# A fixed order for all engines in the heads part of a hybrid block, with the recurrence's growth on VectorE

## The chip, the cores and the metric

One core of one Trainium2 chip runs the kernel. The metric is device microseconds of one execution; three runs of the kernel before gave 1198.59, 1198.85 and 1199.2 us (median 1198.85). Engines are named as in the profile: PE is TensorE's matmul, PEld its weight load, DVE is VectorE, ACT ScalarE, POOL GpSimd, SP SyncE (it issues the weight DMAs).

## The reference, cut to what matters

A block of 512 tokens (with 16 meta tokens: 528) and 1024 channels: half a SwiGLU FFN, a mixer, another half FFN, all in float32. The mixer is the part that is changed.

```python
u = rms_norm(h, mix_norm)
z = u @ w_in                 # 42 blocks of 128 columns
y_a = hgrn2_bidir(...)       # 4 heads: gated linear recurrence, both directions
y_b = axial_gqa(...)         # 8 query heads, 2 key heads, rotary positions, softmax over 528 keys
mixed = sigmoid(zgate_a) * (y_a @ w_up_a) + sigmoid(zgate_b) * (y_b @ w_up_b)
h = h + mixed @ w_out
```

## The kernel before, in words

Activations lie with channels in partitions and tokens in the free dimension. Every float32 product by a weight is made of three matmuls in a reduced format: `Weights.parted` splits a block of weights into a rounded part `whi` (ACT, L84) and the rest `wlo` (DVE, L85), the activations are split the same way into `xh`, `xl`, and `group` (L197) sums hi*hi, hi*lo and lo*hi over eight slices in a PSUM bank. Such matmuls are called weight matmuls here.

The mixer with heads has five strands:

- The main strand: `zcols` computes 128 columns of `z` after another (24 weight matmuls of 512 tokens, or 48 of half the width for 528 tokens) and evicts them on DVE.
- The queries (`queries_rest`): a reciprocal root by Newton steps on DVE, the rotation, a split into `qst`.
- The attention, 32 times (4 pairs of heads, 2 heads each, 4 blocks of 128 queries). `score`: four matmuls fill the one tile `S` (two PSUM banks, a single buffer); DVE takes the maximum (`nm`, L699), ACT scales it (`nr`, L701) and takes the exponentials with their sum (`pr`, L704), DVE inverts the sum (`sm`, L706), ACT scales (`pr`, L707). `turned`: five transposes into `at` and `am`, `ph` on ACT (L722), `pl` on DVE (L723). After four of them `product` multiplies by the values (L734, L735).
- The recurrence of a head (`gla_head`): seven levels m = 1, 2, ... 64. In a level ACT copies `ks` (L884), PE multiplies (L888, tile `gs`, one bank), and `grow` updates: POOL multiplies the query half of Z (L875), DVE the key half (L877), POOL the factors `tot` (L879); DVE writes the level into `A` (L892).
- Its end (`gla_out`): transposes of Z (L916, L921), two sums of states (L926, L928), the output (L942), four squares on ACT (L946), a Newton root on DVE (L561 to L563), four scalings on ACT (L949), a transpose (L953).

Who is next: PE's order is fixed while the program is made. `Interleave` holds a clock that grows by given costs per eight, or 24, weight matmuls, and a strand's step is put into PE's order when its own time (a constant such as LAT_S0 = 3.2 after the last step, LAT_G = 3.5 for a level, LAT_N = 7.0 for the root) has come. `need` runs strands until a condition holds, without main work between: before the queries of head pair hd the scores of hd - 2 must be out, before the recurrence's inputs of hd its head hd - 2 must be done (two buffers of Z). ACT, DVE and POOL are not in this order: a list scheduler with priorities orders them. All engines run their own queues in order, each instruction waiting for its semaphores.

Of the kernel before, what the change touches and what calls it, by code (L numbers as in the profile page):

```python
# [30 lines left out]
OFFSET = 300  # L31
# [20 lines left out]
class Weights:  # L52


    def __init__(self, nc, pool, ahead):
        self.nc, self.pool, self.ahead = nc, pool, ahead
        self.todo, self.ready = [], []
        self.plain = self.into = self.extra = None

# [3 lines left out]
    def emit(self, halves=False):  # L63
# [12 lines left out]
        self.parted(self.pool, [(c, raw[:, c]) for c in cuts])  # L76

# [47 lines left out]
    def fill(self):  # L125
        while self.todo and len(self.ready) <= self.ahead:
            self.emit()
# [6 lines left out]
class Interleave:  # L134
# [3 lines left out]
    def __init__(self, tc, offset):  # L138
        self.tc, self.offset = tc, offset
        self.t, self.chains, self.events, self.done = 0.0, [], {}, set()  # L140

    def add(self, gen):
        self.chains.append([gen, 0.0, None])

    def signal(self, name, latency):
        self.events[name] = self.t + latency

    def ready(self, ch):
        if ch[2] is not None:
            return max(ch[1], self.events.get(ch[2], float("inf")))  # L150
        return ch[1]

    def step(self, ch):
        ch[2] = None
        with self.tc.high_priority(self.offset):
            got = next(ch[0], None)
        if got is None:
            self.chains.remove(ch)
        elif isinstance(got, str):
            ch[2] = got  # L160
        else:
            cost, latency = got
            self.t += cost
            ch[1] = self.t + latency

    def pump(self):
        while True:
            ch = min(self.chains, key=self.ready, default=None)
            if ch is None or self.ready(ch) > self.t:
                return  # L170
            self.step(ch)

    def main(self, cost):
        self.t += cost
        self.pump()

    def need(self, name):
        while name not in self.done:
            ch = min(self.chains, key=self.ready)
            self.t = max(self.t, self.ready(ch))  # L180
            self.step(ch)


def block_kernel(tc, xT, wg1, wu1, wd1, w_in, wup, wout, wg2, wu2, wd2, params,
                 cosT, sinT, masks, ident_in, out):
    nc = tc.nc
    act, dve, pe, pool = nc.scalar, nc.vector, nc.tensor, nc.gpsimd
# [14 lines left out]
    with (tc.tile_pool(name="persist", bufs=1) as sp, tc.tile_pool(name="wts", bufs=1) as wp,  # L202
# [271 lines left out]
        with tc.tile_pool(name="f1", bufs=1) as ft:  # L474
# [45 lines left out]
            plan += tiles[:EARLY] + tiles[KT:KT + 1] + tiles[EARLY:KT] + tiles[KT + 1:]  # L520
# [7 lines left out]
        with tc.tile_pool(name="mix", bufs=1) as mp, tc.manual_schedule(engines={pe.engine}):  # L528
            il = Interleave(tc, OFFSET)

            def zcols(n):

                if n == T:
                    outs = [(bank("mm")[:, :c.stop - c.start], c) for c in FULL]
                else:
                    outs = [(bank("mm"), slice(0, SEQ))]
                group(outs, W.next(), um, il.main)
                return outs

            def scaled(dst, outs, sign=None):  # L540
                for o, cols in outs:
                    if sign is None:
                        dve.tensor_tensor(dst[:, cols], o, R[:, cols], ALU.mult)
                    else:
                        dve.scalar_tensor_tensor(dst[:, cols], o, sign, R[:, cols], ALU.mult, ALU.mult)

            def tmp():
                return mp.tile([P, TP], F32, name="tm", tag="tm", bufs=3)[:, :T]

            def rsqrt(x, scale, eps, shape, tag):  # L550


                x0 = x
                x, y, a = (mn.tile(shape, F32, name=n, tag=n, bufs=b)
                           for n, b in ((f"x{tag}", 1), (f"y{tag}", 2), (f"a{tag}", 1)))
                dve.tensor_scalar(x, x0, scale, eps, ALU.mult, ALU.add)
                yi = y.bitcast(I32)
                dve.tensor_scalar(yi, x.bitcast(I32), 1, None, ALU.logical_shift_right)
                dve.tensor_scalar(yi, yi, -1, 0x5F3759DF, ALU.mult, ALU.add)
                for _ in range(3):  # L560
                    dve.tensor_tensor(a, y, y, ALU.mult)  # L561
                    dve.scalar_tensor_tensor(a, a, -0.5, x, ALU.mult, ALU.mult)
                    dve.scalar_tensor_tensor(y, a, 1.5, y, ALU.add, ALU.mult)  # L563
                return y
# [21 lines left out]
            with tc.tile_pool(name="heads", bufs=1) as hp, tc.tile_pool(name="small", bufs=1) as mn:  # L586
# [6 lines left out]

                def qtmp():
                    return hp.tile([P, TP], F32, name="tq", tag="tq", bufs=1)[:, :T]

                def rope(z, n, cn, cs):

                    zs = qtmp()
                    dve.stream_shuffle(zs[:, :n], z[:, :n], swap)  # L600
                    dve.scalar_tensor_tensor(z[:, :n], z[:, :n], par[:, cn:cn + 1], cosS[:, :n], ALU.mult, ALU.mult)
                    dve.scalar_tensor_tensor(zs[:, :n], zs[:, :n], par[:, cs:cs + 1], sinS[:, :n], ALU.mult, ALU.mult)
                    dve.tensor_tensor(z[:, :n], z[:, :n], zs[:, :n], ALU.add)

# [3 lines left out]
                def keys():  # L608
                    kz = tmp()
                    scaled(kz, zcols(T))  # L610
                    ksq = tmp()
                    act.activation(ksq, kz, AF.Square)
                    il.signal("keys", LAT_SQ)
                    inputs["keys"] = kz, ksq

                def keys_rest():
                    kz, ksq = inputs["keys"]
                    krs = tmp()
                    for cols in FULL:
                        o = bank("mm")  # L620
                        n = cols.stop - cols.start
                        pe.matmul(o[:, :n], kones, ksq[:, cols], start=True, stop=True)
                        act.activation(krs[:, cols], o[:, :n], AF.Sqrt, bias=eps, scale=1.0 / 64)  # L623
                    for cols in FULL:
                        dve.reciprocal(krs[:, cols], krs[:, cols])
                    rope(kz, T, C_KN, C_KNS)
                    dve.tensor_tensor(kz, kz, krs, ALU.mult)
                    for kv in range(2):
                        s, d = slice(kv * 64, kv * 64 + 64), slice(64 - kv * 64, 128 - kv * 64)
                        kh = hp.tile([P, TP], F32R, name=f"kh{kv}")[:, :T]  # L630
                        kl = hp.tile([P, TP], F32R, name=f"kl{kv}")[:, :T]
                        act.copy(kh[s], kz[s])
                        act.copy(kh[d], kz[s])
                        dve.tensor_tensor(kl[s], kz[s], kh[s].bitcast(F32), ALU.subtract)
# [4 lines left out]
                def values():  # L639
                    vz = tmp()  # L640
                    scaled(vz, zcols(T))
                    inputs["values"] = vz
                    il.signal("values", LAT_V)

                def values_rest():
                    vz = inputs["values"]
# [3 lines left out]
                    for cs in (slice(0, 4), slice(4, 5)):  # L650
                        ov = bank("mm").rearrange("p (c v) -> p c v", c=4)
                        w, n = (4, P) if cs.start == 0 else (1, META)
                        for c in range(w):
                            c0 = (cs.start + c) * P
                            pe.transpose(ov[:n, c, :], vz[:, c0:c0 + n], ident)
                        for kv in range(2):
# [451 lines left out]
```

## Time and profile before

| | |
|---|---|
| median of 3 runs | 1198.85 us |
| the profiled execution | 1199.99 us, span 1198.1 us |
| PE busy | 1169.3 us (98% of the span) |
| DVE, ACT, POOL busy | 853.7, 581.4, 186.1 us |
| chain that ended last, by engine | PE 86%, DVE 8%, ACT 2%, issue 2% |

The busy shares say that PE sets the pace; what can be won or lost by an order are the times in which PE waits, and the time in which its clock is granted at the lower of its two levels. The part with heads lies at 381 to 706 us of the span: `rstd` before it ends at 381 us, the transpose L953 of the last head at about 706 us. A busy matmul is modelled at its end, so a short wait can hide in it.

### The profile page before, as it was taken

Reading aid. Unit: us, or ns where it says so; the run is one execution under the profiler, and the core shown is the slowest. Engines: PE = TensorE matmul, PEld = TensorE weight load, DVE = VectorE, ACT = ScalarE, POOL = GpSimd, SP = SyncE. Lnnn points to the kernel's source line nnn. Section 1 sums busy time; section 2 is a strip of 40 time slices with the busy share of each in tenths; the row PEclk is TensorE's granted clock in tenths of the full one; section 3 lists DMA queues with packets and bytes.
Section 4 is the critical chain, followed back from the end, with each engine's and each line's share of the span. In section 5 each row is a group of like instructions: output and inputs, shape, how many; then the busy total and the mean of one; then the engine's idle time right before and its main releaser. Section 6 shows DMA issues by size and latency. Waiting matters only on the chain.

```text
span 1198.1 us, 19412 instructions
## 1 busy us (share of the span) xinstructions
PE 1169.3 (98%) x7765; PEld 1070.7 (89%) x7765; DVE 853.7 (71%) x1349; ACT 581.4 (49%) x982; POOL 186.1 (16%) x153
## 2 busy tenths in 40 slices
PE   8999999999999999899999999999999999999998
PEld 8999999999999788878888788888878998998997
DVE  7988848847956769687677835454788956866863
ACT  5545525524645476656547533334444633543541
POOL 1001001001102023233232410122001101101100
PEclk9999999999999999999999999999999999999999
DMA  6133322323223221111111113232413232333213
GB/s 233 63 95 128 102 89 89 114 80 106 71 67 119 81 71 36 53 37 53 36 54 36 62 45 114 85 117 90 156 53 128 97 102 97 109 98 110 89 54 123
DMA packets 34235, 106.22 MB, mean 89 GB/s; under 512 B 3937, under 2 KB 4321, under 8 KB 34145
## 3 DMA queue, kind: packets, MB, share of 16 engines
q1 hardware_dynamic: 33984, 104.44, 26.0%
q8 instruction: 61, 1.00, 0.3%
q0 software_dynamic: 160, 0.54, 0.1%
q14 instruction: 30, 0.24, 0.1%
HBM read 102.87 MB, written 2.10 MB: 88 GB/s over the span
## 4 chain that ended last, share of the span: by engine, by line
PE 86%; DVE 8%; ACT 2%; issue 2%; DMA 1%; SPq 0%; POOL 0%; ACTq 0%; DVEq 0%
PE mm L197 34%; PE mm L374 14%; PE at L374 9%; PE at L197 5%; PE am L197 5%; PE gs L374 4%; PE S L197 4%; PE am L374 2%; DVE wlo L85 2%; PE gs L888 2%; PE S L695 1%; PE mm L734 1%; PE mm L942 1%; PE at L719 1%; ACT whi L84 1%
## 5 line engine op out<-in xcount | busy, mean ns | idle before, releaser
L84 ACT CAST whi<-raw 128x1024 fp32r<-128x1024 f32 (+2 forms) x220 | 189.4, 862 | 290.5 <-PE mm L197 125.8
L85 DVE TENSOR_TENSOR wlo<-raw,whi 128x1024 fp32r<-128x1024 f32 (+2 forms) x220 | 223.5, 1018 | 28.8 <-ACT whi L84 23.1
L197 PE MATMUL mm<-xh,whi 128*128 128x512 f32 (+1 forms) x504 | 166.3, 363 | 4.7 <-ACT xh L278 1.4
L197 PE MATMUL mm<-xl,whi 128*128 128x512 f32 (+1 forms) x504 | 160.3, 352 | 1.3 <-DVE xl L279 1.3
L197 PE MATMUL mm<-xh,wlo 128*128 128x512 f32 (+1 forms) x504 | 159.4, 350 | 0.0
L116 POOL TENSOR_TENSOR sums<-raw 128x512 f32<-128x512 f32 x36 | 57.9, 1609 | 494.8 <-DVE wlo L85 494.8
L84 ACT CAST whi<-sums 128x1024 fp32r<-128x1024 f32 x72 | 75.4, 1050 | 62.4 <-DVE sums L111 21.2
L85 DVE TENSOR_TENSOR wlo<-sums,whi 128x1024 fp32r<-128x1024 f32 x72 | 87.5, 1217 | 25.2 <-ACT whi L84 25.1
L197 PEld LDWEIGHTS mm<-xh,whi 128*128 128x128 f32 x504 | 89.6, 191 | 17.5 <-ACT tm L623 1.8
L197 PEld LDWEIGHTS mm<-xh,wlo 128*128 128x128 f32 x504 | 89.3, 190 | 12.7 <-issue 0.2
L197 PEld LDWEIGHTS mm<-xl,whi 128*128 128x128 f32 x504 | 89.3, 190 | 11.8 <-DVE xl L279 2.2
L875 POOL TENSOR_TENSOR Z<-Z,tot 128x512 f32<-128x512 f32 x32 | 47.3, 1477 | 157.8 <-PE gs L888 125.1
L197 PE MATMUL mm<-hh,wlo 128*128 128x256 f32 (+1 forms) x218 | 63.0, 334 | 0.0
L197 PE MATMUL mm<-hh,whi 128*128 128x256 f32 (+1 forms) x218 | 62.9, 333 | 0.1
L197 PE MATMUL mm<-hl,whi 128*128 128x256 f32 (+1 forms) x218 | 62.9, 332 | 0.0
L374 PE MATMUL mm<-xl,whi 128*128 128x264 f32 (+1 forms) x216 | 61.3, 284 | 0.0
L374 PE MATMUL mm<-xh,whi 128*128 128x264 f32 (+1 forms) x216 | 61.2, 284 | 0.0
L374 PE MATMUL mm<-xh,wlo 128*128 128x264 f32 (+1 forms) x216 | 61.2, 283 | 0.0
L468 DVE SCALAR_TENSOR_TENSOR h<-mm,h 128x512 f32<-128x512 f32 (+2 forms) x40 | 20.9, 544 | 41.6 <-PE mm L197 41.6
L877 DVE TENSOR_TENSOR Z<-Z,tot 128x528 f32<-128x528 f32 (+1 forms) x32 | 32.5, 1014 | 13.4 <-PE gs L888 9.9
L374 PE MATMUL at<-xh,whi 128*128 128x264 f32 (+1 forms) x144 | 42.0, 291 | 0.0
L197 PEld LDWEIGHTS mm<-hh,wlo 128*128 128x128 f32 x218 | 37.2, 188 | 4.5 <-DVE wlo L85 0.7
(365 smaller groups left out, 3376.8 us busy)
## 6 DMA issues: line engine op xcount, KB each, us to landing
raw<-in_wg SPq DMA_DIRECT2D x43, 512.0 KB, 3.6
raw<-in_wu SPq DMA_DIRECT2D x43, 512.0 KB, 3.3
raw<-in_w_in SPq DMA_DIRECT2D x42, 512.0 KB, 3.2
raw<-in_wd SPq DMA_DIRECT2D x48, 384.0 KB, 3.1
raw<-in_wd SPq DMA_DIRECT2D x16, 256.0 KB, 2.6
raw<-in_wup SPq DMA_DIRECT2D x16, 256.0 KB, 2.6
raw<-in_wout SPq DMA_DIRECT2D x8, 512.0 KB, 3.5
h<-in_xT SPq DMA_DIRECT2D x4, 528.0 KB, 6.5
```

The source lines that it names most:

```text
L84: nc.scalar.copy(hi[:, c], src)
L85: nc.vector.tensor_tensor(lo[:, c], src, hi[:, c].bitcast(F32), ALU.subtract)
L116: nc.gpsimd.tensor_tensor(t[:, E], r0[:, E], r1[:, E], ALU.add)
L197: pe.matmul(o, a[:, sl], b[:, cols], start=(k == 0 and i == 0), stop=(k == n - 1 and i == 2))
L374: pe.matmul(o, a[:, sl], b[:, kk, :], start=(start and kk == 0 and i == 0), stop=(kk == 3 and i == 2), skip_group_check=True)
L468: dve.scalar_tensor_tensor(h[c][:, cols], o, 0.5, h[c][:, cols], ALU.mult, ALU.add)
L695: pe.matmul(s[:, WIDE][:, cols], st[e][:, c * P:(c + 1) * P], kk[:, cols], start=(i == 0), stop=(i == 1))
L719: pe.transpose(o[:, k, :], pr[:, k * P:(k + 1) * P], ident)
L734: pe.matmul(av, v[:, k, :], p[:, k, :], start=(k == 0 and i == 0), stop=False)
L875: pool.tensor_tensor(xx, xx, first, ALU.mult)
L877: dve.tensor_tensor(y, y, second, ALU.mult)
L888: pe.matmul(s[:, c, :], ks[:, c * P:(c + 1) * P], ap(Z, T + c * P, ((2 * m, P // (2 * m)), (T + m, 2), (1, m))), start=True, stop=True)
```

## The change

`Interleave` with its constants goes. `Order` takes its place: every call of `act`, `dve`, `pe` and `pool` passes a wrapper (`Timed`), which adds the instruction's length by a formula to a model of its engine's queue, and to the time at which its strand is ready. A strand now yields at each change of engine, and the one that is ready first goes on. In the part with heads ACT, DVE and POOL are taken from the list scheduler too: their order is the order in which the model makes them. The weights are loaded one block ahead and split as a strand of their own. In `grow`, and in three more products, POOL's work moves to DVE; for m up to 8 the key half and the query half become one instruction of 1056 elements. The sigmoids of the first seven gates come after the attention. Since every call goes through the wrapper, the rows of the kernel after have its line, L276.

```diff
-LAT_S0, LAT_S1, LAT_P, LAT_G, LAT_Q, LAT_K = 3.2, 0.3, 2.5, 3.5, 8.0, 10.0
-LAT_SQ, LAT_R, LAT_V, LAT_O, LAT_N = 4.0, 5.0, 3.0, 1.8, 7.0
...
+class Order:
+    HOP, DRAIN = 0.12, 0.3
...
+    def account(self, eng, op, args, kw):
...
+        if eng == "pe":
+            if cur is not self.main:
+                self.t = max(self.t, cur.ready)
...
+        if eng == "act":
+            d = n * 0.000916 + 0.115
+            if "accum_out" in kw:
+                d += 0.19
...
+        else:
+            d = (n + 160) / 960
+        start = max(self.free.get(eng, 0.0), cur.ready + (self.HOP if cur.eng != eng else 0.0))
+        self.free[eng] = cur.ready = start + d
...
+    def need(self, cond):
+        while not cond():
+            ch = min(self.chains, key=self.ready)
+            r = self.ready(ch)
+            assert r < float("inf"), "nothing can go on"
+            self.t = max(self.t, r)
+            self.step(ch)
...
+            with (tc.tile_pool(name="heads", bufs=1) as hp, tc.tile_pool(name="small", bufs=1) as mn,
+                  tc.manual_schedule(engines={act.engine, dve.engine, pool.engine})):
...
                     def grow(m):
-                        pool.tensor_tensor(xx, xx, first, ALU.mult)
-                        y = ap(Z, 0, ((T, 2), (2 * m, n), (1, m)))
-                        dve.tensor_tensor(y, y, second, ALU.mult)
+                        if n * 2 * m == T:
+                            z = ap(Z, 0, ((2 * T + m, 2), (2 * m, 2 * n), (1, m)))
+                            by = ap(tot, m, ((-m, 2), (2 * m, 2 * n), (0, m)))
+                            dve.tensor_tensor(z, z, by, ALU.mult)
+                        else:
+                            for z0, t0 in ((0, m), (2 * T + m, 0)):
+                                z = ap(Z, z0, ((T, 2), (2 * m, n), (1, m)))
+                                dve.tensor_tensor(z, z, ap(tot, t0, ((T, 2), (2 * m, n), (0, m))), ALU.mult)
...
-                        pool.tensor_tensor(a, a, b, ALU.mult)
+                        dve.tensor_tensor(a, a, b, ALU.mult)
...
+                                yield lambda: out_of[0] < 2
+                                s = wide("S")
...
                 for hd in range(1, HEADS):
                     if hd > 1:
-                        il.need(f"att{hd - 2}")
+                        il.need(lambda: f"att{hd - 2}" in il.done)
                     queries(hd)
```

Place 1 is PE's queue at the end of the second head's recurrence, from the output (`mm<-st,Z`) to the transpose of the scaled output (`mm<-ident,on`); `S<-` are scores, `mm<-ph,vs` the product by the values, `xh,whi` and the like weight matmuls. Before:

```order
L942 MATMUL mm<-st,Z 128x128
L695 MATMUL S<-kh_4664,qst 128x256
...
L197 MATMUL mm<-xh,wlo 128x512
L719 MATMUL at<-ident,pr 128x128 x4
L720 MATMUL am<-ident,pr 16x128
...
L734 MATMUL mm<-ph,vs_4757 128x512
...
L735 MATMUL mm<-pmeta,vs_4757 128x512
L850 MATMUL gs<-ident,tm 128x128 x4
L695 MATMUL S<-kh_4664,qst 128x256
...
L953 MATMUL mm<-ident,on 128x128 x4
```

and now:

```order
L276 MATMUL mm<-st,Z 128x128
L276 MATMUL S<-kh_4791,qst 128x256
L276 MATMUL S<-kh_4791,qst 128x272
L276 MATMUL S<-kl_4792,qst 128x256
L276 MATMUL S<-kl_4792,qst 128x272
L276 MATMUL mm<-ph,vs_4836 128x512
L276 MATMUL mm<-pl,vs_4836 128x512
...
L276 MATMUL mm<-pmeta,vs_4836 128x512
L276 MATMUL mm<-ident,on 128x128 x4
L276 MATMUL mm<-xh,whi 128x512
```

Between the two ends there stood two scores, a set of transposes, one product, the transposes of `tm` and 24 weight matmuls; now one score and one product stand there, and no weight matmul.

Place 2 is DVE's queue from the third score's maximum (`nm<-S`) to the fourth's, in the first pair of heads; `pl<-at,ph` is the attention's, `A<-msk,gs` and `Z<-Z,tot` the recurrence's. Before:

```order
L699 TENSOR_REDUCE nm<-S 128x1
L543 TENSOR_TENSOR tm<-mm,R 128x256
L85 TENSOR_TENSOR wlo<-raw,whi 128x1024
L706 RECIPROCAL sm<-sm 128x1
L543 TENSOR_TENSOR tm<-mm,R 128x272
L723 TENSOR_TENSOR pl<-at,ph 128x4x128
L699 TENSOR_REDUCE nm<-S 128x1
```

and now:

```order
L276 TENSOR_REDUCE nm<-S 128x1
L276 TENSOR_TENSOR Z<-zi,tot 128x512
L276 RECIPROCAL sm<-sm 128x1
L276 TENSOR_TENSOR tm<-mm,R 128x512
L276 TENSOR_TENSOR pl<-at,ph 128x4x128
L276 TENSOR_TENSOR Z<-Z,tot 128x2x528
L276 TENSOR_TENSOR tot<-tot 128x528
L276 COPY_PREDICATED A<-msk,gs 128x512
L276 TENSOR_TENSOR wlo<-raw,whi 128x1024
L276 TENSOR_REDUCE nm<-S 128x1
```

A whole level of the recurrence, with the two products that were POOL's, now stands between two maxima.

## Rows read from the trace of the kernel before

**Rows 1.** Windows, PE at its pace: length, busy time (instructions) by engine, clock, DMA share, GB/s.
```profile
750.00:800.00 50.00, 50.00 (x220) 40.98 (x219) 23.53 (x31) 17.32 (x25) 10.01 (x6) 1.00 0.29 100
1100.00:1150.00 50.00, 50.00 (x412) 49.61 (x411) 44.67 (x60) 28.48 (x45) 9.19 (x5) 1.00 0.26 90
```

**Rows 2.** Timeline, 485 to 487 us: a product's end, eight float32 records, then a score.
```profile
485.26 0.50 PE L735 MATMUL mm<-pmeta,vs 48*128 48x512 f32 x1
...
485.69 1.16 PE L899 MATMUL gs<-Z 128*128 128x128 f32 x8
486.61 0.49 PE L695 MATMUL S<-kh,qst 128*128 128x256 f32 x2
```

**Rows 3.** Windows over the part with heads, 381 to 706 us.
```profile
381.00:426.00 45.00, 42.05 (x259) 36.98 (x257) 32.85 (x63) 19.57 (x33) 2.17 (x7) 1.00 0.27 94
426.00:656.00 230.00, 216.76 (x1390) 191.12 (x1389) 175.84 (x330) 150.08 (x292) 69.73 (x66) 0.98 0.13 47
656.00:706.00 50.00, 47.94 (x251) 39.70 (x250) 33.08 (x41) 23.09 (x37) 18.31 (x16) 1.00 0.15 54
```

**Rows 4.** PE's waits from 381 to 706 us: first and last of 13 lines.
```profile
PE S L695 <- DVE qst L685: 4.8, 2, 2.6
...
PE gs L888 <- ACT ks L884: 0.2, 1, 0.2
```

**Rows 5.** Windows behind PE's three longest waits (the clock is the third number from the end).
```profile
491.90:495.30 3.40, 3.15 (x17) 3.18 (x18) 2.87 (x5) 0.62 (x2) 2.62 (x2) 0.56 0.02 5
535.00:538.50 3.50, 3.32 (x12) 2.76 (x13) 2.77 (x9) 0.69 (x3) 0.00 (x0) 0.62 0.02 5
604.00:607.50 3.50, 3.31 (x10) 2.82 (x11) 3.37 (x8) 0.62 (x1) 0.66 (x1) 0.52 0.12 48
```

**Rows 6.** DVE's groups by form, 380 to 710 us: busy, mean ns, idle before.
```profile
L85 DVE TENSOR_TENSOR wlo<-raw,whi 128x1024 fp32r<-128x1024 f32 x33 | 40.4, 1224 | 3.7 <-ACT whi L84 3.6
L699 DVE TENSOR_REDUCE nm<-S 128x1 f32<-128x528 f32 x32 | 22.4, 701 | 7.2 <-PE S L695 7.0
L723 DVE TENSOR_TENSOR pl<-at,ph 128x512 fp32r<-128x512 f32 x32 | 21.9, 685 | 16.4 <-ACT ph L722 12.9 <-PE mm L735 3.4
L892 DVE COPY_PREDICATED A<-msk,gs 128x512 f32<-128x512 uint8 x28 | 20.6, 735 | 0.0
L877 DVE TENSOR_TENSOR Z<-Z,tot 128x528 f32<-128x528 f32 x16 | 17.3, 1079 | 3.5 <-PE gs L888 3.4
...
L563 DVE SCALAR_TENSOR_TENSOR yo<-ao,yo 128x4 f32<-128x4 f32 x9 | 1.5, 161 | 0.3
```

**Rows 7.** Line L877: shortest, median and longest ns, first and last start, forms.
```profile
L877 DVE TENSOR_TENSOR Z<-Z,tot x32: 681/710/2024, 447.5 to 695.6; 128x528 f32<-128x528 f32 x16, 128x512 f32<-128x512 f32 x16
```

**Rows 8.** Timeline, 496 to 499 us: one score from its last matmul on.
```profile
496.17 0.41 PE L695 MATMUL S<-kl,qst 128*128 128x256 f32 x2
...
496.80 0.70 DVE L699 TENSOR_REDUCE nm<-S 128x1 f32<-128x528 f32 x1
...
497.53 0.29 ACT L701 ACTIVATE nr<-nm,yq 128x1 f32<-128x1 f32 x1 [0.82 <-DVE nm L699]
...
497.86 0.79 ACT L704 ACTIVATE pr<-S,nr,yq 128x528 f32<-128x528 f32 x1
...
498.55 0.19 ACT L704 ACTIVATION_READ_ACCUMULATOR pr<-S,nr,yq 128x1 f32 x1
```

**Rows 9.** ACT's groups by form, 380 to 710 us.
```profile
L707 ACT ACTIVATE pr<-pr,sm 128x528 f32<-128x528 f32 x32 | 23.5, 735 | 7.8 <-DVE sm L706 7.7
L722 ACT CAST ph<-at 128x512 fp32r<-128x512 f32 x32 | 18.5, 579 | 9.2 <-PE mm L734 4.7 <-PE at L719 4.5
L884 ACT COPY ks<-Z 128x512 f32<-128x512 f32 x28 | 18.5, 660 | 29.4 <-DVE Z L877 20.7 <-POOL Z L875 6.2 <-DVE sm L706 2.0
...
L946 ACT ACTIVATE on<-mm 128x128 f32<-128x128 f32 x16 | 4.2, 277 | 9.6 <-PE mm L942 9.6
L949 ACT ACTIVATE on<-mm,yo 128x128 f32<-128x128 f32 x12 | 3.4, 358 | 1.0 <-DVE yo L563 1.0
```

More of the change, by code (lines that the diff above doesn't have):

```diff
@@ L142, in add @@
     def add(self, gen):
-        self.chains.append([gen, 0.0, None])
-    def signal(self, name, latency):
-        self.events[name] = self.t + latency
+        self.chains.append(Chain(gen, self.cur.ready))
     def ready(self, ch):
-        if ch[2] is not None:
-            return max(ch[1], self.events.get(ch[2], float("inf")))
-        return ch[1]
+        return ch.ready if ch.wait is None or ch.wait() else float("inf")
     def step(self, ch):
[L154 to L157, printed above, removed]
-            self.chains.remove(ch)
[L159 to L164, printed above, removed]
+        before, self.cur = self.cur, ch
@@ L166, in pump, with tick @@
+        ch.wait = None
+        try:
+            ch.wait = next(ch.gen)
+        except StopIteration:
+            self.chains.remove(ch)
+        self.cur = before
     def pump(self):
-        while True:
-            ch = min(self.chains, key=self.ready, default=None)
-            if ch is None or self.ready(ch) > self.t:
+        while self.chains:
+            ch = min(self.chains, key=self.ready)
+            if self.ready(ch) > self.t:
                 return
             self.step(ch)
-    def main(self, cost):
-        self.t += cost
+    def tick(self, _=None):
@@ new lines, in zcols, with mm, give, weights @@
+                    outs = [(mm(), slice(0, SEQ))]
+                group(outs, w, um, il.tick)
+                return outs
+            def mm():
+                if state["fifo"]:
+                    il.take()
+                return bank("mm")
+            def give():
+                if state["fifo"]:
+                    il.give()
+            def weights():
+                if not state["fifo"]:
+                    return W.next()
+                il.need(lambda: W.ready)
+                w = W.ready.pop(0)
+                if not W.ready:
+                    if not W.ahead_raw:
+                        W.fetch()
+                    il.main.ready, il.main.eng = il.t + 0.5, "pe"
+                    il.add(W.parts(act, dve))
+                    il.need(lambda: not W.ahead_raw)
+                    W.fetch()
+                return w
@@ L661, in values_rest @@
+                        give()
+                        yield
                     for v in VS:
                         act.copy(v[32:32 + META, 4, :], v[:META, 4, :].bitcast(F32))
[L664 to L670 removed]
@@ L782, in attention @@
[L782 to L791 removed]
+                                yield lambda: waiting
@@ new lines, in turned @@
+                                yield
+                            yield lambda: il.banks and out_of[0] < 3
+                            av, v = mm(), VS[j // 2]
+                            for k in range(4):
+                                for i, p in enumerate((ph, pl)):
+                                    pe.matmul(av, v[:, k, :], p[:, k, :], start=(k == 0 and i == 0), stop=False)
+                            pe.matmul(av, v[:32 + META, 4, :], pmeta, start=False, stop=True)
+                            d, s = slice(e * 64, e * 64 + 64), slice(64 - e * 64, 128 - e * 64)
@@ L1008, in block_kernel, with gate, branch @@
                     dve.tensor_tensor(m, b, sgs[c], ALU.mult)
+                    give()
+                    il.done.add(f"b{c}")
                     mixb.append(m)
-                il.need(f"gla{HEADS - 1}")
+                il.need(lambda: f"gla{HEADS - 1}" in il.done)
+                il.need(lambda: not il.chains)
+                Timed.clock = None
+                state["fifo"] = False
+            def gate(sg):
+                (o, _), = zcols(SEQ)
+                dve.tensor_tensor(sg, o, R[:, :SEQ], ALU.mult)
+                act.activation(sg, sg, AF.Sigmoid)
+            def branch(y):
+                b = bank("mm")
+                group([(b, slice(0, SEQ))], W.next(), y)
+                return b
             with tc.tile_pool(name="tail", bufs=1) as hp:
```

576 lines of the change are left out of this document (344 added, 232 removed).

## The prediction

> **What bounds the kernel now.** I read the page's busy shares first: PE is busy 98% of the span. Then PE at its pace: 220 matmuls of 512 columns in 50 us are 0.227 us each, 412 of 264 and 256 columns 0.121 us each [rows 1]. Eight records of float32 matmuls of 128 columns hold PE for 0.9 us until the next one starts, 485.69 to 486.61 us, so 0.112 each; I count transposes so too, a set of four and a short one at 0.47. A product ends with a matmul of 0.43 us (485.26 to 485.69) [rows 2], in all 8 x 0.227 + 0.43 = 2.25 us. A score's four matmuls take 4 x 0.121 = 0.49 us. The amount of PE work is not changed, so only PE's waits and its clock can move the time.
>
> The windows show where it waits: 45.00 - 42.05 = 2.95 us before the first score, 230.00 - 216.76 = 13.24 us in the middle window, which holds the scores from first to last, and 50.00 - 47.94 = 2.06 us behind, 18.25 us in all [rows 3]. The waits go to 13 pairs, each a step that stood in PE's queue a little ahead of its input: the longest group is 4.8 us in 2 pieces, the shortest 0.2 us [rows 4]. Behind the three longest pieces the mean granted clock of windows of 3.4 to 3.5 us is 0.56, 0.62 and 0.52 [rows 5]: the lower of its two levels (1.2 GHz for 2.4) for most of them. 3.4 us at half speed cost 1.7 us, the three 5.1 us. So 13.2 + 5.1 = 18.3 us of the middle window are open to a better order, and that is about all there is to win.
>
> DVE is busy 175.84 of the 230 us there and POOL 69.73 [rows 3]. On average, then, DVE has room for POOL's work. Whether it has it where PE waits is the question.
>
> **The change, part by part.** Prices first. An instruction on DVE with 512 elements takes 0.685 us and one with 1024 takes 1.224 [rows 6], so the merged growth of 1056 elements is estimated at 1.26 us from these two, and the unmerged pair is 2 x 0.685 = 1.37. The growth of the key half alone had a mean of 1.079 us for the 528-element form [rows 6], but 0.681 at the shortest and 0.710 in the median, 2.024 at most [rows 7]. I take the median, since without POOL's work nothing is left beside it, and so all DVE work at its undisturbed length. Were the excess the strided form's own, a level would cost 1.079 - 0.710 = 0.37 us more, 3 us on the seven levels of a head.
>
> One page bears on that choice. The Trainium skill ("SBUF — State Buffer", section "SBUF: two separate sides") says that VectorE and GpSimd share a port pair by an exclusive lock and that the loser stands still for the whole instruction; by it the excess goes with POOL, as I assume, and the sum is the one below; without it, it is 3 us a head worse. The trace's median of 0.710 beside the maximum of 2.024 [rows 7] agrees with a wait now and then rather than with a slow form.
>
> A score's chain: its last matmul starts at 496.17, the maximum at 496.80 (0.70 us), the scaled maximum at 497.53 (0.29), the exponentials at 497.86 (0.79), the read of their sum at 498.55 (0.19) [rows 8]. S has one buffer, so the next score's matmuls can start at 498.74 at the earliest, 2.6 us later; with the three matmuls before it, 2.8 us from score to score. ACT spends 0.29 + 0.98 + 0.735 + 0.579 = 2.6 us on each [rows 8, 9]. The model in the change counts 0.12, 0.79, 0.60 and 0.58 for these (its formula is in the diff): 0.5 us too little a score, so it puts steps in early.
>
> Now the order, counted between scores 1 to 32. In the new order they stand in bunches, because main work goes ahead while the strands wait for DVE in the model, and `need` then runs strands with no main work left between.
>
> *Scores 2 to 9.* PE: 42 weight matmuls 9.5 us, 7 scores 3.4, 7 sets of transposes 3.3, eight groups of the recurrence 7.1, a product 2.25, the queries' sums 0.45: 26 us. Between the same scores stand 150 weight matmuls before (72 wide, 78 narrow, 25.8 us), 41 us in all. DVE now: per score 0.70 + 0.16 + 0.685, seven times 10.8; seven levels, growth 9.2, factors 2.2, writing A 5.2; the start of the head 2.1; a query's twelve Newton steps of 0.16 and six wide steps 6.0; two weight splits 2.45; two evictions, `pmeta` and `yb` 2.7: 40.5 us [rows 6]. DVE has 14.4 us more than PE, and PE cannot go round it, since each score waits for the maximum of the one before. Place 2 shows one such piece.
>
> *Scores 9 to 16.* PE 25.8, ACT 26.9, DVE 19.9. DVE can carry at most 25.8 - 19.9 = 5.9 us of its backlog into this, so the two stretches lose at least 14.4 - 5.9 = 8.5 us; at most 14.4 and the 9.5 that the next stretch's working gives. I take 15.
>
> *Scores 17 to 24, and again 25 to 32 with the same rows.* PE 25.4, DVE 22.5, ACT 25.8. Place 1 lies in them: from the output to the transpose of the scaled output four squares of 0.277 us and the read of a sum, 0.19, make 1.87 us, twelve Newton steps 1.92, four scalings 1.43 [rows 6, 8, 9], three hand-overs of about 0.1: 5.5 us. PE has 0.49 + 2.25 = 2.75 between: at least 2.75 us of waiting. Before, two scores, two sets of transposes, a product and 24 weight matmuls stood there, half of them narrow: 0.98 + 0.92 + 2.25 + 4.18 = 8.3 us. Further, the maximum of score 18 stands behind 4.5 us of evictions, a weight split and a level; three distances of 2.07 to 2.79 us are no longer than a score's 2.8; and the model's 0.5 us a score is missing. Working the four queues through row by row I get some 35 us against 25.4, or 12 us of loss if each hand-over takes 0.1 us. Bounds 2.75 and 12; I take 8 each, nearer to the worked rows.
>
> *Scores 16 to 17 and 24 to 25* are main work with a recurrence beside it: PE 40.6 and DVE 40.5, then PE 34.4 and DVE 38.5. DVE is full all along: 1.5 (0 to 4) and 4 (1 to 7).
>
> *Behind score 32* the last recurrence has 3.6 us from level to level (0.9 and twelve weight matmuls) for a chain of 0.9, a growth of 1.26, a copy of 0.66 [rows 9] and three hand-overs of some 0.1: 3.1; the main work covers it, and DVE has 51 of 64 us to do. Where a weight split stands in front it costs up to 1 us, no more than the 2.06 that goes. Ahead of score 1 the kinds of waits stay. The order in both FFNs and behind the heads stays. POOL's freed time hides nothing.
>
> *Clock.* The piece of some 3 us at place 1 comes three times (in the first head 3.5 us of work stand where 5.5 are needed). Such pieces were followed by the low clock three times out of three [rows 5]: 3 x 1.7 = 5.1 us (0 to 8.5).
>
> The sum on the profiled execution, 1199.99 us: -18.3, +15, +8, +8, +1.5, +4, +5.1 = +23.3, so 1223 us. It lies 1.1 us over the runs' median, so 1222 on that scale. The low ends give 8.5 + 2 x 2.75 + 1 = 15, less 18.3: -3, 1196. The high ends 24 + 24 + 4 + 7 + 8.5 - 18.3 = +49, 1248.
>
> **Rivals.** (a) *The order works,* the other side: the lengths in the model are mostly those of the trace, and the 13 pairs of waits are all steps that stood too early [rows 4]. In the middle window then 13 to 18 us go: 1181 to 1186, faster. It decides where DVE's work between two scores is no longer than PE's. Against it: that is not so from score 2 to 9, and no queue meets place 1 in 2.75 us.
> (b) *An even trade:* the bunches lose only their low ends, since DVE and ACT run behind and catch up in the next stretch: 1194 to 1201. For it: DVE has slack in the bunches. Against: the single S ties PE to DVE at every score.
> (c) *The chains are worse:* in a bunch each strand waits for the other's queue (a cast for a matmul, that for a cast), nearly all upper ends come together: 1240 to 1252. For it: ACT has 25.8 us to do in 25.4.
> (d) *DVE gets no faster without POOL:* growth stays at its mean; 3 us more for each of three heads, 1231; inside the forecast's own range.
>
> **Chances.** Forecast (1201 to 1240) 0.68, with (d) in it; (a) 0.09; (b) 0.10; (c) 0.13. Faster and no change are told apart at 0.2%, 2.4 us, about what a measurement of this kernel can tell. Of (b) half is faster and half within: faster 0.09 + 0.05 = 0.14, same 0.05, slower 0.68 + 0.13 = 0.81. The range 1197 to 1246 leaves out (a) and the far end of (c).
>
> **What would show it.** Right: PE's busy share falls in the part with heads, its waits there rise to 40 us or more; the largest are scores, transposes of `pr` and levels waiting for DVE, and `mm<-ident,on` waits 2 to 4 us three times with the clock at the lower level behind; DVE is 90% busy between scores 2 and 9 and between 24 and 25; growth of 1056 elements takes about 1.26 us. Wrong: PE waits less than 18 us there, or scores stand under 2.8 us apart in the bunches.

## The result, and the profile after

The kernel after takes 1242.09 us (median of 4 runs, 1240.62 to 1242.71), the kernel before in the same session 1198.72 (1198.46 to 1199.2): a ratio of 1.036, 95% interval 1.0342 to 1.0378, 43 us slower. The profiled execution has a span of 1240.1 us, against 1198.1. The prediction was 1222 with a range of 1197 to 1246: sign and range hold, the size is too small by 20 us. From the first score to the thirty-second the kernel before needed 232.9 us (655.1 - 422.2), the kernel after 257.9 (682.7 - 424.8), although 14.8 us of PE work have moved out of this stretch, mostly behind the last score.

The first line of the page after: busy time, share and instructions of each engine.

```profile
PE 1185.0 (96%) x7765; PEld 1077.0 (87%) x7765; DVE 870.3 (70%) x1409; ACT 577.1 (47%) x979; POOL 100.0 (8%) x77
```

PE's busy share fell from 98 to 96%, and DVE, which took over 86 us of POOL's work, is hardly busier than before. The windows between the scores 2, 9, 16, 17, 24, 25 and 32 of the kernel after (columns as in [rows 1]):

```profile
434.90:480.40 45.50, 33.67 (x190) 27.55 (x188) 35.88 (x69) 25.64 (x50) 0.00 (x0) 0.92 0.11 34
480.40:521.90 41.50, 34.19 (x195) 28.11 (x194) 20.51 (x48) 23.09 (x56) 0.00 (x0) 0.88 0.04 13
521.90:568.50 46.60, 43.45 (x252) 36.87 (x253) 34.80 (x64) 20.48 (x29) 0.18 (x2) 1.00 0.18 57
568.50:604.50 36.00, 28.77 (x195) 24.15 (x194) 23.87 (x55) 22.62 (x55) 0.00 (x0) 1.00 0.08 30
604.50:645.40 40.90, 37.10 (x223) 31.64 (x223) 32.78 (x61) 19.33 (x28) 0.44 (x2) 1.00 0.16 53
645.40:682.70 37.30, 30.16 (x196) 25.65 (x195) 24.00 (x55) 23.07 (x56) 0.00 (x0) 0.95 0.09 29
```

In the four bunches (first, second, fourth, sixth row) PE is busy 74 to 82% of the time, and no other engine is full either: DVE 49 to 79%, ACT 56 to 63%. Each engine waits for another. PE's waits from 381 to 750 us, total, times, longest; they answer to [rows 4]:

```profile
PE gs L276 <- DVE A L276: 17.1, 15, 3.7
PE at L276 <- DVE pl L276: 6.6, 6, 1.8
PE mm L276 <- ACT on L276: 4.0, 2, 2.0
PE at L276 <- ACT pr L276: 3.1, 6, 0.7
PE gs L276 <- ACT ks L276: 2.7, 3, 2.2
...
PE mm L276 <- DVE zg L276: 2.0, 1, 2.0
PE mm L276 <- ACT st L276: 2.0, 1, 2.0
PE S L276 <- ACT pr L276: 1.6, 4, 0.5
```

The largest group are levels of the recurrence that wait until DVE has written the level before into `A`. The longest of them, 3.7 us, shows how it comes about. Timeline of the kernel after, 461 to 470 us:

```profile
461.98 1.13 PE L276 MATMUL gs<-Z,ks 128*128 128x128 f32 x8 [0.85 <-DVE A L276]
462.58 0.71 DVE L276 TENSOR_REDUCE nm<-S 128x1 f32<-128x528 f32 x1
...
463.32 0.69 DVE L276 TENSOR_TENSOR qst<-tm,qst 64x512 fp32r<-64x512 f32 x1
...
463.66 0.79 ACT L276 ACTIVATE pr<-S,nr,yq 128x528 f32<-128x528 f32 x1
...
464.57 0.16 DVE L276 RECIPROCAL sm<-sm 128x1 f32<-128x1 f32 x1 [0.56 <-ACT pr L276]
...
464.77 0.74 ACT L276 ACTIVATE pr<-pr,sm 128x528 f32<-128x528 f32 x1 [0.23 <-DVE sm L276]
...
465.53 0.58 ACT L276 COPY ta<-mm 64x512 f32<-64x512 f32 x1
466.14 0.68 DVE L276 TENSOR_TENSOR yb<-mm,ta 64x512 f32<-64x512 f32 x1 [1.41 <-ACT ta L276]
466.75 1.24 DVE L276 TENSOR_TENSOR Z<-Z,tot 128x1056 f32<-128x1056 f32 x1
...
468.21 0.72 DVE L276 COPY_PREDICATED A<-msk,gs 128x512 f32<-128x512 uint8 x1
...
469.08 1.83 PE L276 MATMUL gs<-Z,ks 128*128 128x128 f32 x7 [3.73 <-DVE A L276]
```

The level's matmuls are done at about 463 us and its growth could start. It starts at 466.75: in DVE's queue the reciprocal `sm` and the sum `yb` stand ahead of it, and both wait for ACT, while DVE is idle for 0.56 and 1.41 us. ACT in turn copies `ta` only behind the exponentials and the scaling of `pr`. So PE waits for DVE, DVE for ACT, and ACT for its own queue, with no engine full.

### The profile page after: what moved, and what is told of

Read it like the earlier page. It is cut to its first block, busy times and chain, and to the rows that moved or that the text cites. A ratio compares the mean times of both kernels' runs of the same rounds, so it can differ in the third digit from the quotient of the medians.

```text
span 1240.1 us, 19340 instructions
## 1 busy us (share of the span) xinstructions
PE 1185.0 (96%) x7765; PEld 1077.0 (87%) x7765; DVE 870.3 (70%) x1409; ACT 577.1 (47%) x979; POOL 100.0 (8%) x77
## 3 DMA queue, kind: packets, MB, share of 16 engines
q1 hardware_dynamic: 33984, 104.44, 26.1%
## 5 line engine op out<-in xcount | busy, mean ns | idle before, releaser
L101 ACT CAST whi<-raw 128x1024 fp32r<-128x1024 f32 (+2 forms) x179 | 150.0, 839 | 251.7 <-PE mm L294 88.6
L102 DVE TENSOR_TENSOR wlo<-raw,whi 128x1024 fp32r<-128x1024 f32 (+2 forms) x179 | 177.6, 995 | 20.6 <-ACT whi L101 18.6
L276 PE MATMUL mm<-xh,whi 128*128 128x512 f32 (+1 forms) x352 | 115.5, 365 | 0.0
L276 PE MATMUL mm<-xl,whi 128*128 128x512 f32 (+1 forms) x352 | 109.2, 348 | 0.0
L276 PE MATMUL mm<-xh,wlo 128*128 128x512 f32 (+1 forms) x352 | 109.0, 347 | 0.0
L101 ACT CAST whi<-sums 128x1024 fp32r<-128x1024 f32 x72 | 75.4, 1050 | 62.4 <-DVE sums L128 20.9
L276 PEld LDWEIGHTS mm<-xh,wlo 128*128 128x128 f32 x352 | 62.3, 192 | 8.2
L276 PEld LDWEIGHTS mm<-xh,whi 128*128 128x128 f32 x352 | 62.9, 193 | 7.3 <-issue 0.7
L276 PEld LDWEIGHTS mm<-xl,whi 128*128 128x128 f32 x352 | 62.7, 193 | 5.4
L276 ACT CAST whi<-raw 128x1024 fp32r<-128x1024 f32 (+1 forms) x41 | 39.4, 965 | 36.9 <-PE mm L276 27.8
L294 PE MATMUL mm<-xh,whi 128*128 128x512 f32 (+2 forms) x152 | 51.4, 365 | 2.7 <-ACT xh L375 2.7
L276 DVE TENSOR_TENSOR wlo<-raw,whi 128x1024 fp32r<-128x1024 f32 (+1 forms) x41 | 45.8, 1116 | 9.8 <-ACT whi L276 9.6
L294 PE MATMUL mm<-xl,whi 128*128 128x512 f32 (+2 forms) x152 | 51.8, 367 | 0.0
L294 PE MATMUL mm<-xh,wlo 128*128 128x512 f32 (+2 forms) x152 | 51.2, 363 | 0.0
```

The lines of the kernel that those rows point to most:

```text
L101: nc.scalar.copy(hi[:, c], src)
L102: nc.vector.tensor_tensor(lo[:, c], src, hi[:, c].bitcast(F32), ALU.subtract)
L276: return f(*args, **kw)
L294: pe.matmul(o, a[:, sl], b[:, cols], start=(k == 0 and i == 0), stop=(k == n - 1 and i == 2))
```

## The experiments

Twelve kernels ran. The ratio is to the kernel before of the same session; 1.0% is 12 us.

| run | what | median us | ratio, 95% interval |
|---|---|---|---|
| e1_dve_load | before, products on DVE | 1206.37 | 1.0056 (1.0040 to 1.0073) |
| e2_list | after, list scheduler for ACT, DVE, POOL | 1227.38 | 1.0235 (1.0218 to 1.0252) |
| e3_pool | after, products back on POOL | 1258.48 | 1.0493 (1.0471 to 1.0515) |
| e4_lengths | after, ACT's lengths corrected | 1238.32 | 1.0321 (1.0306 to 1.0337) |
| e5_gates | after, four gates moved ahead | 1240.28 | 1.0339 (1.0323 to 1.0355) |
| e6_quarter | after, growth cut to a quarter | 1223.97 | 1.0205 (1.0190 to 1.0220) |
| e7_queries | before, queries at normal priority | 1200.79 | 1.0009 (1.0000 to 1.0018) |
| e8_paced | after, scores paced | 1234.48 | 1.0285 (1.0268 to 1.0303) |
| e9_evict | after, `A` ahead of `tot` | 1246.86 | 1.0388 (1.0372 to 1.0403) |
| e10_paced_list | e8 and e2 | 1228.90 | 1.0237 (1.0222 to 1.0253) |
| e11_paced_list_lengths | e10 and e4 | 1220.62 | 1.0173 (1.0158 to 1.0187) |
| e12_load_queries | e1 and e7 | 1195.94 | 0.9972 (0.9959 to 0.9985) |

**The products on DVE: e1, e3, e7, e12.** In e1 the kernel before keeps its order, and POOL's products go to DVE:

```diff
-                        pool.tensor_tensor(xx, xx, first, ALU.mult)
...
-                        dve.tensor_tensor(y, y, second, ALU.mult)
...
+                        if n * 2 * m == T:
...
+                            dve.tensor_tensor(z, z, by, ALU.mult)
+                        else:
+                            for z0, t0 in ((0, m), (2 * T + m, 0)):
...
+                                dve.tensor_tensor(z, z, ap(tot, t0, ((T, 2), (2 * m, n), (0, m))), ALU.mult)
...
-                        pool.tensor_tensor(a, a, b, ALU.mult)
+                        dve.tensor_tensor(a, a, b, ALU.mult)
```

> The kernel before with only the second part of the change: all products of POOL in the heads part (the query half of the growth, the factors tot, ks, Z1, zg) go to DVE, the two halves merged where they can be; PE's order rules and the list scheduler stay as they were. Theory A (the loss comes from the order: what stands between two scores, and in which queue position): the load alone costs little, 1195 to 1206 us, and the mean of the growth falls to its undisturbed length. Rival B (DVE's load itself makes PE wait): 1222 us or more, with waits of PE for DVE over 35 us in the part with heads.

Measured 1206.37, 0.4 above theory A's range and far from B's 1222. PE's longest waits of e1:

```profile
PE S L695 <- DVE qst L685: 8.9, 2, 4.6
PE S L695 <- ACT pr L704: 5.7, 2, 4.8
```

Both hang on the rest of the queries' work, which the kernel before gives the lowest priority of all: with more work on DVE it comes later. e7 takes that priority away from the kernel before, e12 from e1:

```diff
-                        with tc.high_priority(-2 * OFFSET):
-                            queries_of[j] = queries_rest(j)
+                        queries_of[j] = queries_rest(j)
```

> The kernel before, with the one line changed that puts the rest of the queries' work on DVE and ACT behind everything else (lowest priority): now at the priority of its place. If the two waits of scores for qst (4.8 us in before) and the low clock behind two of them (3.4 us) are only this priority: 1190 to 1195 us. If the queries' steps then stand in front of the attention's and the recurrence's and make those late: 1198 to 1204 us.

> e1 (the kernel before with POOL's products on DVE) and e7 (the rest of the queries no longer at the lowest priority) together. In e1 the waits for qst and for the exponentials that the queries hold up are 14.6 us, against 4.8 for qst before. If these are all that the load on DVE costs: 1198 to 1202 us, as e7. If the load costs elsewhere: 1205 to 1210 us, as e1.

e7 gave no gain: one wait for qst is left with 2.5 us, and levels waiting behind ACT's qst and ks take the place of the other. e12 gave 1195.94, faster than both kernels; the theory had 1198 at best. Its two longest groups of waits:

```profile
PE gs L889 <- DVE A L893: 2.7, 1, 2.7
PE S L695 <- DVE qst L685: 2.7, 1, 2.7
```

So all that the load on DVE cost was one priority, and without that it is worth 0.4% (0.9972 against 1.0009). e3 asks the same from the other side, in the new order:

```diff
+        elif eng == "pool":
+            d = 0.0026 * n + 0.15
...
-                            dve.tensor_tensor(z, z, by, ALU.mult)
...
+                        pool.tensor_tensor(xx, xx, first, ALU.mult)
...
+                        dve.tensor_tensor(y, y, second, ALU.mult)
...
```

> The kernel after, with the growth's query half, the factors tot and the other three products back on POOL (the model counts POOL with 0.0026 us an element and 0.15, by the trace of before, and makes its order anew). Rival B (DVE's load is to blame): DVE has some 26 us less to do in the part with heads, 1215 to 1225 us. Theory A (the order is to blame): bunches stay, 1235 to 1250 us.

Measured 1258.48, slower than either theory had it. The kernel after, with the products on DVE, is faster than e3 by 16 us, not slower. Groups of e3 (POOL's growth, ACT's copy `ks` behind it, DVE's form of 512 elements, then PE's largest wait):

```profile
L278 POOL TENSOR_TENSOR Z<-Z,tot 128x512 f32<-128x512 f32 x32 | 49.0, 1532 | 101.6 <-PE gs L278 93.9 <-ACT ph L278 7.5 <-ACT nr L278 0.2
...
L278 ACT COPY ks<-Z 128x512 f32<-128x512 f32 x28 | 18.5, 660 | 57.2 <-DVE Z L278 30.0 <-POOL Z L278 20.9 <-DVE xq L278 6.2
...
L278 DVE TENSOR_TENSOR Z<-Z,tot 128x512 f32<-128x512 f32 x16 | 13.6, 851 | 2.9 <-PE gs L278 2.8
```

```profile
PE gs L278 <- ACT ks L278: 17.9, 19, 2.6
```

A product takes POOL 1.53 us in e3 and DVE 0.69 in the kernel after, and the level cannot go on before the later half. That half is POOL's in 10 of the 32 growths only. In the other 22 DVE's half ends later; `ks` waits 30.0 us for DVE's half and 20.9 for POOL's. The model also made a new order with POOL's lengths, so the 16 us belong to the products and the new order together, and no run takes them apart.

**The fixed queues: e2.**

```diff
-            with (tc.tile_pool(name="heads", bufs=1) as hp, tc.tile_pool(name="small", bufs=1) as mn,
-                  tc.manual_schedule(engines={act.engine, dve.engine, pool.engine})):
+            with tc.tile_pool(name="heads", bufs=1) as hp, tc.tile_pool(name="small", bufs=1) as mn:
```

> The kernel after, with ACT, DVE and POOL given back to the list scheduler in the part with heads; PE's order stays that of the kernel after, row by row. Theory A1 (the fixed order of ACT's and DVE's queues makes them block one another: a growth stands ready behind a reciprocal that waits for ACT): 1215 to 1230 us. Rival A2 (PE's order with its bunches of scores and levels without main work is to blame, whatever stands in the other queues): 1235 to 1245 us. If the scheduler's order is worse than the model's, over 1245.

Measured 1227.38, inside A1's range. The same PE order with other queues on ACT and DVE is 14.7 us faster, and still 2.35% behind the kernel before. DVE's own waits from 430 to 690 us, in the kernel after:

```profile
DVE sm L276 <- ACT pr L276: 25.7, 23, 1.3
DVE pl L276 <- ACT ph L276: 13.9, 22, 2.8
DVE yb L276 <- ACT ta L276: 11.0, 7, 2.4
```

and in e2:

```profile
DVE pl L276 <- ACT ph L276: 16.3, 21, 2.1
DVE nm L276 <- PE S L276: 11.4, 13, 2.0
DVE sm L276 <- ACT pr L276: 5.4, 7, 1.3
...
DVE yb L276 <- ACT ta L276: 3.6, 3, 1.8
```

The scheduler puts the reciprocal and `yb` where their input has come, with growths ahead of them: 36.7 us of idle DVE become 9.0, and DVE waits for PE's scores instead, 11.4. PE's waits for `A` fall from 17.1 to 0.5 us, but in part only by name, since `tot` now comes last in a level:

```profile
PE gs L276 <- DVE tot L276: 7.0, 6, 1.4
```

All waits of PE's matmuls into the recurrence's tile `gs` fall from 20.9 to 11.8 us; the longest groups are now waits for ACT's `pr`, 8.6 us, and `on`, 7.8. PE's waits together go from 45.0 to 37.2 us. The clock adds to it: from 381 to 750 us it is at its lower level for 13.6 us in e2 and for 23.8 in the kernel after, which makes some 5 us of the 15.5 between the two spans.

**DVE's amount, and one place in its queue: e6, e9.**

```diff
+                        def cut(z, by):
+                            il.account("dve", "tensor_tensor", (z,), {})
+                            z, by = (t[:, :, :, :m // 4] if m >= META else t[:, :, :t.shape[2] // 4] for t in (z, by))
+                            nc.vector.tensor_tensor(z, z, by, ALU.mult)
...
```

> The kernel after in its own order on all engines, but the growth's products on DVE cover a quarter of their elements (the rest of Z is not updated, so the output is not the reference's), about 0.9 us less on DVE for each of 28 levels, 26 us in all. Theory B (DVE's amount of work is what PE waits for): the waits of levels for DVE go, 15 to 25 us less, 1217 to 1227 us. Theory A1 (the growth stands ready behind instructions that wait for ACT): less than half of it, 1230 to 1240 us.

Measured 1223.97, 18 us less: theory B's number. The growth fell to 0.43 us where it was 1.25, and to 0.29 where it was 0.69, 26 us in all; 70% of it came back, and levels waiting for `A` went from 17.1 to 5.8 us. With e1 and e12 this says: DVE's work on the growth counts in the kernel after, while the same work costs nothing in the order of before. The likely reason is that the growth lies on a level's chain and has waited already, but that is argued: e6 shortens a step of the chain and DVE's sum at once, and no run shortens work of DVE that lies off the chain.

```diff
                         ready = il.cur.ready
+                        if evict:
+                            evict()
                         a, b = (ap(tot, i, ((T, 2), (2 * m, n))) for i in (0, m))
                         dve.tensor_tensor(a, a, b, ALU.mult)
...
-                        grown = grow(m)
-                        dve.copy_predicated(A[:, 0], msk[:, None, li * P:(li + 1) * P].broadcast_to([P, 4, P]), s)
...
+                        grown = grow(m, evict)
...
```

Here `evict` is the write into `A` (`copy_predicated`).

> The kernel after, with one step moved in each level of the recurrence: DVE writes the level into A before it multiplies the factors tot, not behind (0.6 us earlier, and the tile gs is free that much earlier). The largest group of PE's waits is levels waiting for that write, 17.1 us in 15 pieces. If the place in DVE's queue makes them: 6 to 10 us less, 1232 to 1236 us. If what stands ahead of the growth makes them (instructions waiting for ACT): 0 to 4 us less, 1238 to 1243 us.

Measured 1246.86, above both ranges: no gain (a ratio of 1.0388 against 1.0360, with intervals that overlap). The waits for `A` are gone, and these are now the largest:

```profile
PE at L276 <- DVE pl L276: 11.4, 10, 2.9
PE gs L276 <- DVE tot L276: 9.6, 10, 3.4
```

The second has taken over the name. All waits of matmuls into `gs` did fall, from 20.9 to 15.9 us, but the first line grew from 6.6 and others with it, to 46.1 us of waits in all, against 45.0. So the place of the write was not what PE waited for in the end; that the growth in front of it was late is the reading of the timeline above, and e9 agrees with it. It is no clean test: the model also made its order anew, and 658 of the 7765 places in PE's queue hold another matmul, while in e2 and e6 all stand as in the kernel after.

**The order of PE and the model: e4, e5, e8, e10, e11.**

```diff
-                d += 0.19
+                d += 0.39 if n > P else 0.25
+            elif f == AF.Copy:
+                d += 0.13 if n > 1 else 0.18
```

> The kernel after, with the lengths of ACT's instructions in the model corrected by the trace (scaling with the sum read out 0.2 us longer, scaled copies 0.13 to 0.18 longer); the order is made anew with them. If steps put in some 0.5 us a score too early are a good part of the loss: 1225 to 1235 us. If the loss is the bunches themselves, which need main work between and not better times: 1237 to 1245 us.

Measured 1238.32, 4 us less: the second theory, near its lower end.

```diff
                 for hd in range(1, HEADS):
                     if hd > 1:
+                        for _ in range(2):
+                            sgs.append(mp.tile([P, SEQ], F32, name="mixb", tag="mb", bufs=4))
+                            gate(sgs[-1])
                         il.need(lambda: f"att{hd - 2}" in il.done)
```

> The kernel after, with four of the gate blocks that follow the heads (24 weight matmuls, 5.4 us each) moved into the bunches of scores 9 to 16 and 17 to 24, two each, ahead of the point where `need` runs the attention alone. Theory A2 (PE waits in the bunches because no main work stands there that could be done meanwhile; 16 of the 43 us more than before are waits in these two bunches): 8 to 15 us less than the kernel after, 1227 to 1234 us. Rival A1 (the waits come from ACT and DVE blocking one another, and last as long whatever PE has beside): 1238 to 1245 us.

Measured 1240.28, inside A1's range, but it did not do what it was to: main work that is not waiting goes ahead at once, so most of the gates landed between scores 16 and 17 (60.4 us instead of 46.6) and 24 and 25 (50.3 instead of 40.9). It settles nothing on the bunches. e8 spreads the main work by holding the scores back:

```diff
                                 yield lambda: out_of[0] < 2
+                                il.cur.ready = max(il.cur.ready, il.last_score + 7.0)
+                                yield
+                                il.last_score = il.t
```

> The kernel after with one rule more in its model: a score is not put in before 7.0 us of the model's time have gone by since the one before (in the kernel before 7.4 us lie between two scores on average). All engines keep a fixed order, DVE all the products. Between scores 9 and 32 the main work then stands spread out (2 to 4 us a score in most places, 8.9 us instead of 30.5 between 16 and 17). e5 did not test the bunches, since most of its moved work landed ahead of them; this does. Theory A2 (the bunches): 10 to 20 us less than the kernel after, 1222 to 1232 us. Rival A1 (ACT's and DVE's fixed queues block one another wherever main work stands): 1236 to 1245 us.

Measured 1234.48, 7.6 us less than the kernel after and between the two theories: the bunches are part of it, and less than half of what A2 had at most. The growth still waits: levels for `A` 11.5 us in 12 pieces.

> The paced order of e8 for PE, with ACT, DVE and POOL given back to the list scheduler. Theory A (both the bunches and the fixed queues cost, and the products on DVE some 7 us): the parts add up to 1205 to 1215 us. If the two are one and the same waits: no better than e2, 1222 to 1230 us.

Measured 1228.90, no better than e2: what the scheduler and the pacing save is largely the same time, so the two do not add. PE's largest group of waits in e10:

```profile
PE at L277 <- ACT pr L277: 17.4, 16, 2.5
```

> e10 (paced order of PE, list scheduler for the rest) with the model's ACT lengths of e4, so that a score's scaled `pr` is expected 0.6 us later. In e10 the largest group of PE's waits is transposes waiting for ACT's scaled `pr`, 17.4 us in 16 pieces. If the model's lengths put those transposes in too early: most of these waits go, 1212 to 1220 us. If they come from the scheduler, which lets ACT do other things first: 1225 to 1231 us.

Measured 1220.62, 0.6 above the first theory's range and well under e10. In e11:

```profile
PE mm L279 <- ACT on L279: 7.3, 3, 4.1
PE gs L279 <- DVE tot L279: 5.9, 4, 2.6
PE at L279 <- ACT pr L279: 4.1, 5, 1.4
```

The transposes had been put in too early by the model's short ACT; 13 of the 17.4 us are gone. Other waits grew, so PE's waits together fell only from 35.4 to 31.4 us; of the 10.0 us between the two spans 6.8 are the clock, at its lower level for 10.2 us from 381 to 750 instead of 23.8. With the scheduler's queues the model's error costs 8 us, with fixed queues 4. The first line is place 1 of the prediction.

Read as steps, before to e1 to e2 to after: products on DVE +0.56% (all of it the queries' priority), the new order of PE with all that came with it (weights split as a strand, the priorities gone, the later sigmoids) +1.8%, the fixed order of ACT, DVE and POOL +1.25%. The steps are not independent, as e10 shows. What stays open: e11, with pacing and corrected lengths, is still 1.2% over e1. Place 1 is 7.3 us of waits in it; no run separates the rest, nor PE's order from what came with it.

## Why the prediction was right in sign and short in size

**The terms.** PE's work by the prediction's own prices, set against the stretches measured (the loss contains the low clock):

| scores | PE work | measured | loss | predicted |
|---|---|---|---|---|
| 2 to 9 and 9 to 16 | 26.1 + 25.8 | 45.5 + 41.5 | 35.1 | 15 |
| 16 to 17 | 40.6 | 46.6 | 6.0 | 1.5 |
| 17 to 24 | 25.4 | 36.0 | 10.6 | 8 |
| 24 to 25 | 34.4 | 40.9 | 6.5 | 4 |
| 25 to 32 | 25.4 | 37.3 | 11.9 | 8 |
| clock | | | (10.2 of these) | 5.1 |

That makes 70 us of loss, against 41.6 predicted. The kernel before by the same prices: 202.9 us of PE work between scores 1 and 32 in 232.9 us, 30.0 lost, where I had let only 18.3 go; the other 11.7 stand in no wait that the view names. (The middle window of the prediction, from 426 us, also begins 4 us behind the first score at 422.2.) 70 - 30 = 40 of the 42 us between the two spans. Both sides were too small, by 28 and by 12, and the errors cancelled in part. That the range held the time is owed to this: with the losses as measured and the win as I had it, the sum would have been 1251 us, outside the range.

**The step that failed is the term for scores 2 to 16:** +15 with an upper end of 24, measured 35.1, or 26.6 without the clock. I took DVE for the engine that is full from 2 to 9 ("90% busy between scores 2 and 9 and between 24 and 25") and let it hand on a backlog that the next stretch carries off beside PE's work. The amount was right: the instructions between the second and the ninth maximum sum to 41.1 us, I had 40.5. Two things were not.

First, DVE was busy 35.9 of 45.5 us (79%), and 32.8 of 40.9 (80%) in the other stretch. It stood still in front of steps that waited for ACT, which a sum of durations does not show. Second, scores 9 to 16 carried nothing off: they lost 15.7 us themselves (10.6 without the clock) with DVE busy 20.5 of 41.5, much as the two later bunches, 10.6 and 11.9, whose queues the prediction had worked through row by row. The upper end of 24 held both losses, 14.4 and 9.5; the 15 did not. e2 takes the two apart. With other queues, nearly the same sum (39.6) and the same PE order, scores 2 to 9 take 36.6 us with DVE 91% busy, but 9 to 16 still 39.3:

```profile
436.00:472.60 36.60, 30.10 (x191) 24.84 (x189) 33.31 (x67) 25.46 (x50) 0.00 (x0) 1.00 0.13 44
472.60:511.90 39.30, 31.00 (x194) 25.99 (x193) 19.97 (x49) 23.30 (x57) 0.11 (x1) 0.91 0.04 14
```

So 11 of the 35.1 us are the fixed queues with their clock, and 24.0 remain in e2 (3.4 of them the clock). What makes up the loss inside a bunch under the scheduler's queues stays open.

**The clock** was mis-sized too: 5.1 with an upper end of 8.5, measured 10.2 between the scores and 1.7 ahead of them. Windows of the kernel after at the lower level, as [rows 5]:

```profile
390.30:393.70 3.40, 3.40 (x18) 3.40 (x17) 2.85 (x12) 0.00 (x0) 0.00 (x0) 0.50 0.36 135
444.90:448.30 3.40, 3.40 (x16) 3.03 (x14) 3.17 (x4) 1.99 (x4) 0.00 (x0) 0.50 0.00 0
468.80:472.20 3.40, 3.12 (x14) 3.08 (x15) 2.47 (x5) 1.63 (x4) 0.00 (x0) 0.50 0.00 0
492.70:499.50 6.80, 6.80 (x31) 6.26 (x30) 3.12 (x6) 3.66 (x10) 0.00 (x0) 0.50 0.00 0
513.10:516.50 3.40, 3.40 (x11) 2.21 (x10) 0.85 (x2) 1.73 (x4) 0.00 (x0) 0.51 0.00 0
677.00:680.40 3.40, 3.40 (x14) 2.94 (x13) 2.27 (x4) 0.98 (x2) 0.00 (x0) 0.50 0.02 5
```

I expected the low clock three times, behind place 1. Four of the five stretches between the scores came between scores 2 and 16, with waits of two levels, a transpose of Z and a product.

**Place 1** was right in kind and too large in size: `mm<-ident,on` waits 2.0 us, the low edge of the 2 to 4 said and under the bound of 2.75 that the sum used; in two heads, not in three, and with the clock low behind one of them.

**The growth** was right: 1.25 us for 1056 elements (1.26 predicted) and 0.69 for 512, on a DVE without POOL beside it, against 1.08 in the mean for the key half before [rows 6]:

```profile
L276 DVE TENSOR_TENSOR Z<-Z,tot 128x512 f32<-128x512 f32 x32 | 20.6, 686 | 3.0 <-ACT nr L276 1.6 <-PE gs L276 1.0 <-issue 0.4
...
L276 DVE TENSOR_TENSOR Z<-Z,tot 128x1056 f32<-128x1056 f32 x16 | 20.0, 1252 | 3.5 <-PE gs L276 3.5
```

Rival (d) falls. With POOL back, in e3, the same 512 elements have a mean of 0.85 us. The Trainium skill ("SBUF — State Buffer", "SBUF: two separate sides") has the two engines exclude one another from a shared port pair; the excess that came and went with POOL agrees with it.

**The waits:** 40 us or more in the part with heads was right, 45 us from 381 to 750. Transposes of `pr` and levels were the largest as said; scores were not, 1.6 us, and the closest two scores stood 3.29 us apart. The model's short ACT was named and is real: 4 us in the fixed queues (e4). Rival (a) is refuted; (c), each strand waiting for the other's queue, describes what happened in the fixed queues better than the forecast's full DVE, and its 1240 to 1252 holds the time, where the forecast's own 1201 to 1240 does not.

## What to carry to other kernels

When an order is fixed on several engines that feed each other, sum no engine's durations alone: follow one result through the queues and ask, of each instruction ahead of it, what that one waits for; an engine at 79% can be the one that everything waits for. A move of work and an order should be tried apart: here the move was worth 0.4% after one priority was lifted, and the order around it, with what came with it, cost 3%. A wait names the last step of a late chain, so look at the step in front too: with the write into `A` moved, the wait came back under another name and others grew.

## What the runs showed of the hardware

Two things were not expected. DVE's instructions overlap: of the 73 between the second and the ninth maximum, 37 begin before the one ahead has ended, by 0.083 us in the mean. The 73 sum to 41.1 us and fill 38.0, so sums from mean durations are a few per cent high. And the clock did not follow the length of a wait from run to run. In the kernel after it fell to its lower level at six of the seven waits of 2.02 to 3.73 us between 381 and 750 us (not at the one at 599 us), and at none of the shorter ones. But in e4 it stayed at its upper level behind a wait of 3.09 us at 593.7, and in e3 it fell at 480.1 us, where from 473 us on PE had only six waits of 0.5 to 0.6 us, 3.3 us together:

```profile
480.10:483.50 3.40, 3.40 (x14) 3.11 (x14) 1.78 (x4) 3.08 (x7) 1.26 (x2) 0.50 0.00 0
```
